# A hybrid decoder block: 128 bytes under the last product's stationary tiles, the first chunk's loads ahead of its gates, and a last norm without GpSimd

## The chip, the cores and the metric

The kernel runs on one core of one Trainium2 chip. The metric is the device time of one execution in microseconds (us), lower is better. A run of this kernel has three timed executions, 1505.19, 1507.73 and 1509.2 us, with a median of 1507.73 us; one more execution was profiled, and it took 1503.95 us.

Names of the engines in what follows: PE is the matrix engine (PEld its loads of the stationary operand), DVE the vector engine, ACT the scalar engine, POOL is GpSimd, SP the engine that here only issues transfers. A "product" is one PE matmul instruction.

## The reference

One decoder layer on 512 rows of 1024 float32 values: a mixer (windowed attention beside gated linear attention), then a retrieval layer over 16384 experts, with a modulated norm before each and a plain norm at the end. The change touches the expert layer's second half and the final norm.

```python
q = (h @ wq).reshape(B, S, PEER_HEADS, 2, PEER_QDIM // 2)
sub_scores = jnp.einsum('bshpk,hpnk->bshpn', q, subkeys)
top_v, top_i = lax.top_k(sub_scores, PEER_TOPK)            # 16 of 128 keys, twice per head
... best 16 of 256 candidate pairs -> expert (row number), gates (softmax)
ub = jnp.take(u, eb, axis=0)                               # 128 rows of u per token
hid = jax.nn.gelu(jnp.einsum('tkd,td->tk', ub, xb), approximate=False) * gb
vb = jnp.take(v, eb, axis=0)                               # 128 rows of v per token
return jnp.einsum('tk,tkd->td', hid, vb)
...
x = x + gate2 * peer_ffn(h2, ...)
return rms_norm(x, final_norm_w)                           # x * rsqrt(mean(x*x) + 1e-6) * w
```

## The kernel before

**Two ways to the experts.** The 512 tokens are four blocks of 128. For the last block (number 3, `GB`) the kernel gathers the rows of u and v that each token asks for: POOL issues 128 indirect transfers of 512 KB for u (`gather_u`, tile `gu`) and 128 for v (`gather_v`, tile `gv`), and DVE turns each into a row of `hid` or adds it to `gacc`. For the other three blocks (`DENSE`) it is dense: PE multiplies all 16384 rows of u with the tokens, in 128 chunks of 128 experts (the U part, tile `ph`, 24 products of 352 columns per chunk), ACT applies gelu and stores it to DRAM (`gsp`), and the gates of the chosen experts, scattered into a dense matrix (`Gd`, written in 24 pieces through `gs`), are multiplied on. The V part then adds, chunk by chunk, the products of (gelu x gate) with the chunk's 128 rows of v into six PSUM banks `acc`, one for each of three blocks and two halves of 512 columns.

**Float32 by parts.** Each operand is split in a high and a low part (`...h`, `...l`, written by ACT and by DVE), and one float32 product is three PE products in `mm3`: high by high (line 70), high by low (71) and low by high (72). In the V part the stationary operand is a 128x128 slice of `Ah` or `Al` (gelu x gate, four tiles each, 1536 bytes per partition and tile), and the moving operand is one half, 512 columns, of `vc..h` or `vc..l`. A V chunk is therefore 3 blocks x 2 halves x 3 = 18 products, and each is preceded by its own load of the stationary operand.

**Order of the V part.** A list `xs` names the chunks left to do: the last odd U chunks, one ahead of every second V chunk as far as they go, then V chunks alone. `prep(i)` puts the work on ACT, DVE and POOL that chunk i needs (multiply gelu by gate at line 1289, split, gather as many rows as `due[i]` asks for), two steps ahead of PE. `loads(i)` issues transfers on SP's queue ahead of need: v (1 MB for two chunks, line 1221), gelu (`gel` for two even chunks, 1227; `geo` for one odd chunk, 1234), gates (`gr`, 1.5 MB for eight chunks, 1244; the first in two halves, one on SP and one on POOL, 1242). A queue issues in order, so a transfer that has to wait holds those behind it. The engines' orders are as written in the code from here on (`manual_schedule`); no planner moves them.

**Where tiles stand.** The tiles of the V part come from the pool `dn` at the upper end of a partition's 229,376 bytes, in which each new name takes the next place. In the built program the four `Ah` tiles start at byte 204,640 and `Al` at 210,784; `vc..h` stands from 88,032 and `vc..l` from 104,416 in another pool.

**The end.** `close_half` (lines 1331 to 1334) takes one PSUM bank: two DVE instructions, then a square with a sum on ACT. `root` makes the mean and the logarithm/exponential root of it (two DVE, two ACT instructions of one column), `refine` a Newton step (DVE, one column), `finish` scales by root and weight and stores. Block 3 is closed while PE still works, at steps counted from `LAST_G`; the last four chunks run block by block, so that block 0 can be closed first, then 1, then 2. Block 1's scaling was on ACT and its multiplication with the weight `fwb` on POOL (line 1441); block 2's on DVE (1444, 1446) ahead of its scale.

Of the kernel before, what the change touches and what calls it, by code (L numbers as in the profile page):

```python
# [7 lines left out]
F32 = mybir.dt.float32  # L8
# [4 lines left out]
AF = mybir.ActivationFunctionType  # L13
OP = mybir.AluOpType
# [3 lines left out]
P = 128  # L18
# [29 lines left out]
def peer_block_kernel(ctx: ExitStack, tc: tile.TileContext, a: dict, out: bass.AP):  # L48
    nc = tc.nc
# [8 lines left out]
    def raw(shape, name):  # L58
        return st.tile(shape, F32, tag="raw", bufs=3, name=name)
# [17 lines left out]
    def rstd_of(pool, ss, n, w, name):  # L77
        m = pool.tile([P, w], F32, name=name + "m", tag="rsm", bufs=2)
        y = pool.tile([P, w], F32, name=name + "y", tag="rsy", bufs=2)
        t = pool.tile([P, w], F32, name=name + "t", tag="rst", bufs=2)  # L80
        nc.vector.tensor_scalar(m, ss, 1.0 / n, EPS, op0=OP.mult, op1=OP.add)
        nc.scalar.activation(y, m, AF.Ln)
        nc.scalar.activation(y, y, AF.Exp, scale=-0.5)
        nc.vector.tensor_tensor(t, y, y, OP.mult)
        nc.vector.tensor_tensor(t, t, m, OP.mult)
        nc.vector.tensor_scalar(t, t, -0.5, 1.5, op0=OP.mult, op1=OP.add)
        nc.vector.tensor_tensor(y, y, t, OP.mult)
        return y
# [94 lines left out]
    for L in LW:  # L183
        m = 64 >> L
# [50 lines left out]
    for n in range(NT):  # L235
# [5 lines left out]
        r = rstd_of(frA, ss[:, 0:1], float(D), 1, f"ra{n}")  # L241
# [927 lines left out]
    dn = ctx.enter_context(tc.tile_pool(name="dn", bufs=1, side="right", reuse_waits="tile"))  # L1169
    pacc = ctx.enter_context(tc.tile_pool(name="pacc", bufs=1, space=PSUM, side="right", reuse_waits="tile"))  # L1170
    acc = [pacc.tile([P, 512], F32, name=f"acc{i}") for i in range(2 * len(DENSE))]
    fwb = dn.tile([P, D], F32, name="fwb")
    gacc = dn.tile([P, D], F32, name="gacc")
    vPc = a["vP"].rearrange("(c i) d -> c i d", i=P)
    LEAD, LAST, LAST_G = 8, 4, 121

    rest = [c for c in range(1, P, 2) if c not in AHEAD]
    xs = [("u", c) for c in rest if c <= LEAD]
# [24 lines left out]
    raws = Ring(lambda name: raw([P, 2, D], name), 3)  # L1203
# [14 lines left out]
    def load_v(ring):  # L1218
        c = vrest.pop(0)
        v = ring.take(f"v{c}", step["v", c + 1])  # L1220
        nc.sync.dma_start(v, vPc[c:c + 2].rearrange("c i d -> i c d"))
        vraw[c], vraw[c + 1] = v[:, 0], v[:, 1]

    def load_gel():
        c = grest.pop(0)
        t = gels.take(f"gel{c}", step["v", c + 2])
        nc.sync.dma_start(t, gsp[c // 4, 0].rearrange("c p t -> p c t"))
        for j in range(2):
            gel[c + 2 * j] = t[:, j].rearrange("p (g t) -> p g t", g=NGU)
# [6 lines left out]
    def load_gates():  # L1236
        j = jrest.pop(0)
        t = gates_r[j] = grs.take(f"gr{j}", step["v", j * CG + CG - 1])
        flat = lambda h: t[h].rearrange("p g c t -> p g (c t)")
        if j == 0:  # L1240
            for h, eng in ((slice(0, 64), nc.sync), (slice(64, P), nc.gpsimd)):
                eng.dma_start(flat(h), Gd[j, h])
        else:
            nc.sync.dma_start(flat(slice(0, P)), Gd[j])

    def loads(i):
        at = lambda x, n: step[x] <= i + n
        if i == 1:
            load_gates()
            load_v(raws)  # L1250
            load_gel()
        if i < 1:
            return
        while True:
            if vrest and at(("v", vrest[0]), 12) and vraws.free(i):
                load_v(vraws)
            elif vrest and not urest and at(("v", vrest[0]), 9) and raws.free(i):
                load_v(raws)
            elif urest and at(("u", urest[0]), 9) and raws.free(i):
                load_u()  # L1260
            elif grest and at(("v", grest[0]), 9) and gels.free(i):
                load_gel()
            elif orest and at(("v", orest[0]), 9) and odds.free(i):
                load_odd()
            elif jrest and at(("v", jrest[0] * CG), 11) and grs.free(i):
                load_gates()
            else:
                break
# [45 lines left out]
    def spare(name):  # L1314
        return gp.tile([P, D], F32, tag="gr", bufs=GR, name=name)

    def spare2(name):
        return dn.tile([P, D], F32, tag="gr2", bufs=G2, name=name)

    def half(t, q):  # L1320
        return t[:, q * 512:(q + 1) * 512]

    gate2b = h2n
    fin = {}
# [5 lines left out]
    def close_half(n, src, q):  # L1330
        y, xr, ss = fin[n][:3]
        nc.vector.tensor_tensor(half(y, q), src, half(gate2b, q), OP.mult)
        nc.vector.tensor_tensor(half(y, q), half(y, q), half(xr, q), OP.add)
        nc.scalar.activation(half(xr, q), half(y, q), AF.Square, accum_out=ss[:, q:q + 1])

    def root(n):
        ss = fin[n][2]
        m, r = ss[:, 2:3], ss[:, 3:4]
        nc.vector.tensor_tensor(ss[:, 0:1], ss[:, 0:1], ss[:, 1:2], OP.add)
        nc.vector.tensor_scalar(m, ss[:, 0:1], 1.0 / D, EPS, op0=OP.mult, op1=OP.add)  # L1340
        nc.scalar.activation(r, m, AF.Ln)
        nc.scalar.activation(r, r, AF.Exp, scale=-0.5)
        fin[n] += [m, r]

    def refine(n):
        m, r = fin[n][3:5]
        t = fin[n][2][:, 4:5]
        nc.vector.tensor_tensor(t, r, r, OP.mult)
        nc.vector.tensor_tensor(t, t, m, OP.mult)
        nc.vector.tensor_scalar(t, t, -0.5, 1.5, op0=OP.mult, op1=OP.add)  # L1350
        nc.vector.tensor_tensor(r, r, t, OP.mult)

    def store(n, q, t, eng=None):
        (eng or nc.sync).dma_start(out[n * P:(n + 1) * P, q * 512:(q + 1) * 512], half(t, q))
# [63 lines left out]
    for b in DENSE[1:]:  # L1418
        for q in range(2):
            v_matmuls(last, (b,), (q,))  # L1420

    n0, n1, n2 = DENSE
    x0, x1 = fin[n0], fin[n1]
    for n, y, xr in ((n0, spare("y0"), x0), (n1, spare2("y1"), x1)):
        fin[n] = [y, xr, dn.tile([P, 5], F32, tag=f"sm{n}", bufs=1, name=f"sm{n}")]
    open_block(n2, spare2("y2"), spare("xf2"))
    w2 = spare("w2")
    close_half(n0, acc[0], 0)
    close_half(n0, acc[1], 1)
    close_half(n1, acc[2], 0)  # L1430
    root(n0)
    refine(n0)
    finish(n0)
    close_half(n1, acc[3], 1)
    close_half(n2, acc[4], 0)
    root(n1)
    refine(n1)
    y1, r1 = fin[n1][0], fin[n1][4]
    for q in range(2):
        nc.scalar.activation(half(y1, q), half(y1, q), AF.Copy, scale=r1)  # L1440
        nc.gpsimd.tensor_tensor(half(y1, q), half(y1, q), half(fwb, q), OP.mult)
        store(n1, q, y1)
    y2 = fin[n2][0]
    nc.vector.tensor_tensor(half(w2, 0), half(y2, 0), half(fwb, 0), OP.mult)
    close_half(n2, acc[5], 1)
    nc.vector.tensor_tensor(half(w2, 1), half(y2, 1), half(fwb, 1), OP.mult)
    root(n2)
    refine(n2)
    r2 = fin[n2][4]
    nc.scalar.activation(half(w2, 0), half(w2, 0), AF.Copy, scale=r2)  # L1450
    store(n2, 0, w2, nc.scalar)
    nc.vector.tensor_scalar(half(w2, 1), half(w2, 1), r2, None, op0=OP.mult)
    store(n2, 1, w2)


# [57 lines left out]
```

## Time and profile before

| what | us |
|---|---|
| median of the timed executions | 1507.73 |
| the profiled execution, its own time | 1503.95 |
| its span, first to last instruction | 1502.2 |
| PE busy in the span | 1451.1 |
| DVE busy | 1262.3 |
| ACT busy | 681.3 |
| POOL busy | 533.8 |
| first V product starts at | 799.59 |
| last V product starts at | 1490.01 |

A "page" is the profile's summary of this one execution; "views" are answers of the trace behind it. In a row of instructions the first number is the start in the span, the second how long it took, then engine, line, kind, "what is written <- what is read" and in brackets the idle time of that engine just before and what ended it. Products are pipelined: each is recorded as longer than the step to the next one's start, and the step is what counts. In a row of a view by stretches stand, for each engine, busy time and number of instructions, then the clock that PE was granted (1.00 is full), the busy share of the transfer engines and what they moved.

### The profile page before, as it was taken

The numbers are of one execution on the slowest core, as the hardware profiler recorded it, in microseconds if no ns is written. First come the engines' busy times: TensorE is split into PE (matmuls) and PEld (weight loads), VectorE is DVE, ScalarE is ACT, GpSimd is POOL, SyncE is SP. The second block draws the span as 40 slices with busy tenths as digits, with TensorE's granted clock in tenths as the row PEclk, the third lists the DMA queues.
The fourth block names the chain that finished last, engine by engine and source line by source line (L and its number), as shares of the span: only waits on it lengthen the run. The fifth ranks groups of instructions, "written<-read, shape, count | busy, mean of one in ns | idle before, by whom it ended". The sixth has DMA issues, their size and how long they took to land.

```text
span 1502.2 us, 24546 instructions
## 1 busy us (share of the span) xinstructions
PE 1451.1 (97%) x9387; PEld 1281.2 (85%) x9387; DVE 1262.3 (84%) x2422; ACT 681.3 (45%) x1073; POOL 533.8 (36%) x360
## 2 busy tenths in 40 slices
PE   4999999899999999999999999999999999999996
PEld 3787877788999999999998888888888888888885
DVE  7578757689999999899956888888888888988886
ACT  5445576533444565566643333333333333433343
POOL 1000000145516444122324555555665656533210
PEclk9999999999999999999999999999999999999998
DMA  9253435353356999799999999999999999999941
GB/s 348 104 212 114 170 94 215 135 187 135 111 184 216 330 347 344 253 318 328 332 294 399 409 364 407 361 372 356 391 372 364 357 404 354 406 407 406 363 161 70
DMA packets 165893, 431.63 MB, mean 287 GB/s; under 512 B 12032, under 2 KB 83984, under 8 KB 153360
## 3 DMA queue, kind: packets, MB, share of 16 engines
q1 hardware_dynamic: 109920, 261.81, 47.7%
q0 software_dynamic: 41552, 151.80, 27.2%
q10 hardware_dynamic: 14304, 16.46, 3.1%
q8 instruction: 73, 1.20, 0.3%
q14 instruction: 44, 0.36, 0.1%
HBM read 385.48 MB, written 44.50 MB: 286 GB/s over the span
## 4 chain that ended last, share of the span: by engine, by line
PE 90%; DVE 4%; ACT 3%; DMA 2%; issue 1%; SPq 0%; DVEq 0%; ACTq 0%
PE acc L71 12%; PE acc L72 12%; PE acc L70 12%; PE ph L70 10%; PE ph L72 10%; PE ph L71 10%; PE pg L929 4%; PE pq L70 2%; PE pq L72 2%; PE pq L71 2%; DMA gel<-gsp 1%; PE pj L72 1%; PE pj L70 1%; PE pj L71 1%; DVE macc L275 1%; PE pn L70 1%
## 5 line engine op out<-in xcount | busy, mean ns | idle before, releaser
L1004 POOL DMA_INDIRECT gu<-in_u_dram,ix_u x128 | 197.1, 1540 | 252.5 <-DVE gu L1014 103.8
L1039 POOL DMA_INDIRECT gv<-in_vP_dram,ix_v x128 | 190.6, 1489 | 177.2 <-DVE gacc L1044 112.1
L1044 DVE SCALAR_TENSOR_TENSOR gacc<-gv,hg,gacc 128x1024 f32<-128x1024 f32 x127 | 162.5, 1280 | 0.2
L1014 DVE SCALAR_TENSOR_TENSOR gu<-gu,h2n 128x1024 f32<-128x1024 f32 x128 | 155.4, 1219 | 2.8 <-DMA gu<-in_u_dram,ix_u 2.8
L706 ACT ACTIVATE ge<-ph 128x352 f32<-128x352 f32 x128 | 57.9, 452 | 202.2 <-PE ph L72 164.1
L970 POOL DMA_INDIRECT spr<-in_u_dram,spix x32 | 72.4, 2263 | 106.4 <-DVE spr L975 69.4
L1293 ACT ACTIVATE Ah<-gr 128x384 fp32r<-128x384 f32 x128 | 66.5, 520 | 93.9 <-DVE gr L1289 93.9
L1094 POOL IOTA iot<- 128x256 bf16 x1 | 1.5, 1542 | 281.5 <-DVE h2Tl L681 281.5
L931 ACT ACTIVATE gs<-pg 128x512 f32<-128x512 f32 x96 | 95.1, 1114 | 0.0
L922 DVE TENSOR_TENSOR o<-o,gp 128x3072 bf16<-128x3072 bf16 x48 | 83.9, 1752 | 0.0
L929 PE MATMUL pg<-o,o 128*128 128x128 bf16 x1152 | 73.6, 219 | 0.0
L929 PEld LDWEIGHTS <-o 128*128 128x128 bf16 x1152 | 66.3, 97 | 5.4
L1302 DVE TENSOR_TENSOR Al<-gr,Ah 128x384 fp32r<-128x384 f32 x128 | 70.6, 551 | 0.0
L906 DVE TENSOR_TENSOR o<-iot,t 128x2048 bf16<-128x2048 bf16 x48 | 58.3, 1220 | 11.1 <-PE pg L929 11.1
L218 DVE SCALAR_TENSOR_TENSOR macc<-wa,scs,macc 128x1024 f32<-128x1024 f32 x28 | 39.3, 1403 | 4.3 <-DMA wa<-in_w_ada_dram 3.9
L975 DVE SCALAR_TENSOR_TENSOR spr<-spr,xs 128x1024 f32<-128x1024 f32 x32 | 39.0, 1220 | 3.6 <-DMA spr<-in_u_dram,spix 3.5
L1289 DVE TENSOR_TENSOR gr<-gel,gr 128x352 f32<-128x352 f32 x64 | 33.2, 519 | 9.4 <-DMA gel<-gsp 9.4
L71 PE MATMUL pq<-h2Tl,wq_0h 128*128 128x512 f32 (+1 forms) x80 | 27.9, 349 | 1.2 <-DVE h2Tl L681 1.2
L70 PE MATMUL pq<-h2Th,wq_0h 128*128 128x512 f32 (+1 forms) x80 | 28.0, 352 | 1.0 <-ACT qha L769 1.0
L71 PE MATMUL pq<-h2Tl,wq_1h 128*128 128x512 f32 (+1 forms) x80 | 28.2, 352 | 0.0
L72 PE MATMUL pq<-h2Th,wq_1l 128*128 128x512 f32 (+1 forms) x80 | 28.1, 351 | 0.0
L70 PE MATMUL pq<-h2Th,wq_1h 128*128 128x512 f32 (+1 forms) x80 | 28.0, 349 | 0.0
(2587 smaller groups left out, 5042.5 us busy)
## 6 DMA issues: line engine op xcount, KB each, us to landing
u<-in_uT_dram SPq DMA_DIRECT2D x64, 1024.0 KB
v<-in_vP_dram SPq DMA_DIRECT2D x64, 1024.0 KB
Gd<-gs SPq DMA_DIRECT2D x23, 1024.0 KB
gr<-Gd SPq DMA_DIRECT2D x15, 1536.0 KB
wa<-in_w_ada_dram SPq DMA_DIRECT2D x20, 1024.0 KB
gsp<-ge ACTq DMA_DIRECT2D x84, 176.0 KB
gel<-gsp SPq DMA_DIRECT2D x32, 352.0 KB
wi<-in_w_in_dram SPq DMA_DIRECT2D x9, 1024.0 KB
```

The costliest lines, as they stand in the source:

```text
L70: nc.tensor.matmul(acc, lh, rh, start=start, stop=False)
L71: nc.tensor.matmul(acc, lh, rl, start=False, stop=False)
L72: return nc.tensor.matmul(acc, ll, rh, start=False, stop=stop)
L922: nc.vector.tensor_tensor(o2, o12[:, :, 1, None].to_broadcast([P, H, 3, P, 2]), gp3[:, g0:g0 + H, :, None].to_broadcast([P, H, 3, P, 2]), ...
L929: nc.tensor.matmul(pt[:, i, :], o12[:, g, 0, :, r], o2[:, g, m, :, r], start=(m == 0), stop=(m == 2))
L931: nc.scalar.activation(gs[:, :, t0 + 4 * f:t0 + 4 * f + 4].rearrange("p b a -> p a b"), pt, AF.Copy)
L970: nc.gpsimd.indirect_dma_start(out=sp[j], out_offset=None, in_=a["u"], in_offset=bass.IndirectOffsetOnAxis(ap=sp["ix"][:, j:j + 1], axis=0))
L1004: nc.gpsimd.indirect_dma_start(out=ur, out_offset=None, in_=a["u"], in_offset=bass.IndirectOffsetOnAxis(ap=ix_u[:, s:s + 1], axis=0))
L1014: nc.vector.scalar_tensor_tensor(ur, ur, 1.0, h2n, op0=OP.mult, op1=OP.mult, accum_out=hid[:, s:s + 1])
L1039: nc.gpsimd.indirect_dma_start(out=vr, out_offset=None, in_=a["vP"], in_offset=bass.IndirectOffsetOnAxis(ap=ix_v[:, s:s + 1], axis=0))
L1044: nc.vector.scalar_tensor_tensor(gacc, vr, hg[:, s:s + 1], gacc, op0=OP.mult, op1=OP.add)
L1302: nc.vector.tensor_tensor(grp(Al), A, grp(Ah), OP.subtract)
```

## The change

1. **Place.** A tile `gap` of 32 float32 (128 bytes) is added to the pool `dn`. In the built program the `Ah` tiles then start at 204,512 and the `Al` tiles at 210,656, 128 bytes lower than before; `vc..h` and `vc..l` stay where they were. Because of point 2, `gel` and `gr` also change places in the pool.
2. **Order of the first loads.** At step 1 `loads` issued the first gates, then the first v, then the first gelu. Now it issues gelu, v, gates.
3. **The last norm.** `refine` multiplies twice in one instruction. Block 0's `root` stands ahead of block 1's first `close_half`, and block 1's `root` ahead of block 2's first. Block 1 is weighted on DVE into a new tile `w1` and scaled on ACT, which also stores it; POOL has no part in it any more.
4. **`LAST_G`** is 122 instead of 121: the 256 gathers are spread up to V chunk 122, and block 3's closing steps come one chunk later.

```diff
-    LEAD, LAST, LAST_G = 8, 4, 121
+    LEAD, LAST, LAST_G = 8, 4, 122
...
     def loads(i):
         if i == 1:
+            load_gel()
+            load_v(raws)
             load_gates()
-            load_v(raws)
-            load_gel()
...
     def refine(n):
-        nc.vector.tensor_tensor(t, r, r, OP.mult)
-        nc.vector.tensor_tensor(t, t, m, OP.mult)
+        nc.vector.scalar_tensor_tensor(t, r, r, m, op0=OP.mult, op1=OP.mult)
         nc.vector.tensor_scalar(t, t, -0.5, 1.5, op0=OP.mult, op1=OP.add)
         nc.vector.tensor_tensor(r, r, t, OP.mult)
+    def weighted(n, q, w):
+        nc.vector.tensor_tensor(half(w, q), half(fin[n][0], q), half(fwb, q), OP.mult)
+    def scaled(n, q, w):
+        nc.scalar.activation(half(w, q), half(w, q), AF.Copy, scale=fin[n][4])
+        store(n, q, w, nc.scalar)
...
+    dn.tile([P, 32], F32, name="gap")
...
+    w1 = spare2("w1")
     close_half(n0, acc[0], 0)
     close_half(n0, acc[1], 1)
+    root(n0)
     close_half(n1, acc[2], 0)
-    root(n0)
     refine(n0)
     finish(n0)
     close_half(n1, acc[3], 1)
+    root(n1)
     close_half(n2, acc[4], 0)
-    root(n1)
+    weighted(n1, 0, w1)
     refine(n1)
-    for q in range(2):
-        nc.scalar.activation(half(y1, q), half(y1, q), AF.Copy, scale=r1)
-        nc.gpsimd.tensor_tensor(half(y1, q), half(y1, q), half(fwb, q), OP.mult)
-        store(n1, q, y1)
-    nc.vector.tensor_tensor(half(w2, 0), half(y2, 0), half(fwb, 0), OP.mult)
+    scaled(n1, 0, w1)
+    weighted(n1, 1, w1)
+    scaled(n1, 1, w1)
+    weighted(n2, 0, w2)
     close_half(n2, acc[5], 1)
-    nc.vector.tensor_tensor(half(w2, 1), half(y2, 1), half(fwb, 1), OP.mult)
+    weighted(n2, 1, w2)
     root(n2)
     refine(n2)
-    nc.scalar.activation(half(w2, 0), half(w2, 0), AF.Copy, scale=r2)
-    store(n2, 0, w2, nc.scalar)
-    nc.vector.tensor_scalar(half(w2, 1), half(w2, 1), r2, None, op0=OP.mult)
+    scaled(n2, 0, w2)
+    nc.vector.tensor_scalar(half(w2, 1), half(w2, 1), fin[n2][4], None, op0=OP.mult)
     store(n2, 1, w2)
```

PE's instructions stand in the same order before and after; only addresses differ. Two places on other engines matter.

The first is SP's queue at the start of the V part, as a difference (u are the last U chunks' weights, `gr` the gates of chunks 0 to 7, `v` and `gel` rows of v and gelu for the first chunks; the numbers at the names' ends are buffers):

```order
 L1215 DMA u_8935<-in_uT_dram 128x2048
-L1242 DMA gr_8946<-Gd 64x3072
-L1221 DMA v_8949<-in_vP_dram 128x2x1024
-L1227 DMA gel_8951<-gsp 128x2x352
+L1227 DMA gel_8946<-gsp 128x2x352
+L1221 DMA v_8948<-in_vP_dram 128x2x1024
+L1242 DMA gr_8950<-Gd 64x3072
 L1221 DMA v_8953<-in_vP_dram 128x2x1024
 L1221 DMA v_8955<-in_vP_dram 128x2x1024
```

The three transfers have swapped their outer two, so that gelu and v no longer stand behind the gates, which must wait for the last piece of `Gd`; the other half of the gates stays where it was on POOL's queue.

The second is DVE at the very end, from the first half of block 2 (`acc_8927`) on. Before (`y_14829` and `sm_14832` are block 2, `sm_14828` block 1):

```order
L1332 TENSOR_TENSOR y_14829<-acc_8927,h2n 128x512
L1333 TENSOR_TENSOR y_14829<-y_14829,xf_14830 128x512
L1339 TENSOR_TENSOR sm_14828<-sm_14828 128x1
L1340 TENSOR_SCALAR sm_14828<-sm_14828 128x1
L1348 TENSOR_TENSOR sm_14828<-sm_14828 128x1
L1349 TENSOR_TENSOR sm_14828<-sm_14828 128x1
L1350 TENSOR_SCALAR sm_14828<-sm_14828 128x1
L1351 TENSOR_TENSOR sm_14828<-sm_14828 128x1
L1444 TENSOR_TENSOR w_14833<-y_14829,fwb 128x512
L1332 TENSOR_TENSOR y_14829<-acc_8928,h2n 128x512
L1333 TENSOR_TENSOR y_14829<-y_14829,xf_14830 128x512
L1446 TENSOR_TENSOR w_14833<-y_14829,fwb 128x512
```

And now, with the same names (`w_14834` is the new `w1`; lines 1348 to 1350 are `refine`, 1353 is `weighted`):

```order
L1339 TENSOR_TENSOR sm_14828<-sm_14828 128x1
L1340 TENSOR_SCALAR sm_14828<-sm_14828 128x1
L1332 TENSOR_TENSOR y_14829<-acc_8927,h2n 128x512
L1333 TENSOR_TENSOR y_14829<-y_14829,xf_14830 128x512
L1353 TENSOR_TENSOR w_14834<-y_14826,fwb 128x512
L1348 SCALAR_TENSOR_TENSOR sm_14828<-sm_14828 128x1
L1349 TENSOR_SCALAR sm_14828<-sm_14828 128x1
L1350 TENSOR_TENSOR sm_14828<-sm_14828 128x1
L1353 TENSOR_TENSOR w_14834<-y_14826,fwb 128x512
L1353 TENSOR_TENSOR w_14833<-y_14829,fwb 128x512
L1332 TENSOR_TENSOR y_14829<-acc_8928,h2n 128x512
L1333 TENSOR_TENSOR y_14829<-y_14829,xf_14830 128x512
```

Block 1's root has moved ahead of block 2's first half, the Newton step is one instruction shorter, and two multiplications with the weight, which POOL made before, stand on DVE ahead of block 2's second half.

More of the change, by code (lines that the diff above doesn't have):

```diff
@@ L1434, in peer_block_kernel @@
     close_half(n1, acc[3], 1)
+    root(n1)
     close_half(n2, acc[4], 0)
-    root(n1)
+    weighted(n1, 0, w1)
     refine(n1)
-    y1, r1 = fin[n1][0], fin[n1][4]
-    for q in range(2):
-        nc.scalar.activation(half(y1, q), half(y1, q), AF.Copy, scale=r1)
-        nc.gpsimd.tensor_tensor(half(y1, q), half(y1, q), half(fwb, q), OP.mult)
-        store(n1, q, y1)
-    y2 = fin[n2][0]
-    nc.vector.tensor_tensor(half(w2, 0), half(y2, 0), half(fwb, 0), OP.mult)
+    scaled(n1, 0, w1)
+    weighted(n1, 1, w1)
+    scaled(n1, 1, w1)
+    weighted(n2, 0, w2)
     close_half(n2, acc[5], 1)
-    nc.vector.tensor_tensor(half(w2, 1), half(y2, 1), half(fwb, 1), OP.mult)
+    weighted(n2, 1, w2)
     root(n2)
     refine(n2)
-    r2 = fin[n2][4]
-    nc.scalar.activation(half(w2, 0), half(w2, 0), AF.Copy, scale=r2)
-    store(n2, 0, w2, nc.scalar)
-    nc.vector.tensor_scalar(half(w2, 1), half(w2, 1), r2, None, op0=OP.mult)
+    scaled(n2, 0, w2)
+    nc.vector.tensor_scalar(half(w2, 1), half(w2, 1), fin[n2][4], None, op0=OP.mult)
     store(n2, 1, w2)
```

## The prediction

> **What bounds the kernel now.** I read the page's busy times first, then the chain that ended last, and then the steps between products in PE's rows in order of time.
>
> ```profile
> PE 1451.1 (97%) x9387; PEld 1281.2 (85%) x9387; DVE 1262.3 (84%) x2422; ACT 681.3 (45%) x1073; POOL 533.8 (36%) x360
> PE 90%; DVE 4%; ACT 3%; DMA 2%; issue 1%; SPq 0%; DVEq 0%; ACTq 0%
> PE acc L71 12%; PE acc L72 12%; PE acc L70 12%; PE ph L70 10%; PE ph L72 10%; PE ph L71 10%; PE pg L929 4%; PE pq L70 2%; PE pq L72 2%; PE pq L71 2%; DMA gel<-gsp 1%; PE pj L72 1%; PE pj L70 1%; PE pj L71 1%; DVE macc L275 1%; PE pn L70 1%
> ```
>
> PE makes 90% of the chain, and the V products (`acc`) 36% of it: about 540 us. What a V product costs PE sets the time, as long as transfers and DVE keep up.
>
> **Part 1, the place of the stationary tiles.** All products here with 512 moving columns do the same arithmetic. Below are, from the rows in order of time, the starts of a product and of the eighteenth after it in four groups (`pj`, `pw`, `pq`, `acc`):
>
> ```profile
> 72.50 0.39 PE L70 MATMUL pj<-hTh,wi_0h 128*128 128x512 f32 x1
> 76.58 0.39 PE L70 MATMUL pj<-hTh,wi_1h 128*128 128x512 f32 x1
> ...
> 246.34 0.39 PE L70 MATMUL pw<-wo2000h,ah 128*128 128x512 f32 x1
> 250.46 0.39 PE L70 MATMUL pw<-wo2000h,ah 128*128 128x512 f32 x1
> ...
> 337.31 0.39 PE L70 MATMUL pq<-h2Th,wq_0h 128*128 128x512 f32 x1
> 341.44 0.39 PE L70 MATMUL pq<-h2Th,wq_1h 128*128 128x512 f32 x1
> ...
> 1205.30 0.39 PE L70 MATMUL acc<-vc66h,Ah 128*128 128x512 f32 x1
> 1209.48 0.40 PE L70 MATMUL acc<-vc67h,Ah 128*128 128x512 f32 x1
> 1209.72 0.39 PE L71 MATMUL acc<-vc67l,Ah 128*128 128x512 f32 x1
> ...
> 1213.68 0.32 PE L70 MATMUL ph<-h2Th,uc77h 128*128 128x352 f32 x1
> ```
>
> Eighteen products take 4.08 us in `pj`, 4.12 in `pw`, 4.13 in `pq`, and 4.20 in a V chunk (4.18 in one that follows a U chunk). What differs is where the operands stand. By the built program's addresses, divided by 512, moving and stationary operand leave 160 and 160 in `pj`, 480 and 160 in `pw`, 288 and 480 in `pq`, 480 and 352 in `acc`. Stationary less moving, again by 512: 0, 192, 192, 384. `pw` and `pq` have no remainder in common but the same difference, and the same time within 0.01 us. So I read it thus: while a product streams, the next one's stationary tile is read, and the two reads disturb each other by the difference of their addresses.
>
> The change makes the difference 256. If the pattern repeats every 256 bytes, that is `pj`'s 0, and a chunk takes 4.08. If it repeats every 512 only, 256 lies between 192 (4.13) and 384 (4.20), by a straight line at 4.15. In units of 256 the groups stand at 0, 192 and 128 with 4.08, 4.13, 4.20: the worst is the one farthest from 0, as a repeating pattern would have it. I take 4.08. Of the 128 chunks 40 follow a U chunk (44 odd chunks are left for this part, four of them run ahead of it): now 88 x 4.20 + 40 x 4.18 = 536.8 us, then 128 x 4.08 = 522.2 us, **-14.6 us**. The bounds are -5.6 (4.15) and, if the guess on addresses is wrong altogether, 0 or a loss, priced below.
>
> The Trainium skill speaks against this part: its page TensorE: Matmul & The Clock Gate, section Step-by-step: what each phase is for, says that PE has two independent read ports and that loading the next stationary tile takes no read bandwidth from the running product. By that rule part 1 brings nothing and the sum is that of the rival "no effect"; the four times above are what the rule leaves unexplained.
>
> Can the rest keep up? While PE only ran V chunks and gathers were at their densest:
>
> ```profile
> DMA packets 65643, 243.09 MB, mean 380 GB/s; under 512 B 5979, under 2 KB 16159, under 8 KB 61251
> ...
> 1300.00:1400.00 100.00, 100.00 (x431) 80.42 (x430) 87.93 (x121) 35.35 (x49) 39.80 (x32) 1.00 1.03 404
> ...
> ACT vc6h L1290 <- DMA v<-in_vP_dram: 4.7, 1, 4.7
> ```
>
> From 800 to 1440 us 243 MB move at 380 GB/s; 14.6 us less asks for 389, and 404 was held over 100 us. The last row is ACT's longest wait for a transfer there, once, early. DVE, 88% busy in the second row, goes to about 90%. Neither becomes the bound.
>
> **Part 2, the first loads.** From the chain, the rows of SP, POOL, DVE and PE, and the view by stretches of 1 us:
>
> ```profile
> 773.23 6.03 DMA Gd<-gs
> 779.32 0.49 SPq L1242
> ...
> 791.94 0.94 POOL L1039 DMA_INDIRECT gv<-in_vP_dram,ix_v  x1 [2.08 <-DMA gr<-Gd]
> ...
> 795.03 1.06 ACT L1290 ACTIVATE vc0h<-v 128x1024 fp32r<-128x1024 f32 x1 [4.33 <-DMA v<-in_vP_dram]
> ...
> 798.46 0.53 DVE L1289 TENSOR_TENSOR gr<-gel,gr 128x352 f32<-128x352 f32 x1 [9.40 <-DMA gel<-gsp]
> ...
> 797.39 0.32 PE L71 MATMUL ph<-h2Tl,uc9h 128*128 128x352 f32 x1
> 797.55 0.32 PE L72 MATMUL ph<-h2Th,uc9l 128*128 128x352 f32 x1
> 799.59 0.49 PE L70 MATMUL acc<-vc0h,Ah 128*128 128x512 f32 x1 [1.72 <-ACT Ah L1293]
> 806.03 0.39 PE L70 MATMUL acc<-vc1h,Ah 128*128 128x512 f32 x1
> ...
> 802.00:803.00 1.00, 1.00 (x4) 0.71 (x4) 1.00 (x3) 0.88 (x1) 0.00 (x0) 0.50 1.04 418
> ```
>
> The gates wait for the last piece of `Gd` until 779.32; v and gelu stand behind them and land at 795 and 798. PE, free at 797.71 (797.55 and a step of 0.16), starts at 799.59, 1.88 us late, and its first chunk takes 6.44 us instead of 4.18, because low parts come late and, after the idle time, the granted clock is 0.50: 2.26 us more. Together 4.1 us.
>
> Now gelu and v go out right behind the last u, before 773, and the gates are last. Both halves had landed by 791.94, when POOL's next gather was let go. The 1.4 MB moved ahead can hold up `Gd` and with it the gates, at 404 GB/s by 3.5 us, to 795.4. From gates to PE it is 799.59 - 798.46 = 1.13 us, so PE could start at 796.5, before it is free. **-4.1 us**; the bound is 0, if `Gd` is held up some 3 us more. POOL's gathers behind its half of the gates move by the same 3.5 us at most.
>
> On the clock, the same page of the Trainium skill, section HAM oscillation — how this bites in real kernels, lets PE idle for about 3.4 us before it is slowed; by that rule only the idle 1.88 us and the late parts were to be had here, but the row at 802 shows the slower clock after 1.88 us.
>
> **Part 3, the last norm.** DVE's rows, with one of ACT and POOL each:
>
> ```profile
> 1482.07 0.69 DVE L1332 TENSOR_TENSOR y<-acc,h2n 128x512 f32<-128x512 f32 x1 [0.73 <-PE acc L72]
> 1486.71 0.68 DVE L1332 TENSOR_TENSOR y<-acc,h2n 128x512 f32<-128x512 f32 x1
> 1488.04 0.68 DVE L1332 TENSOR_TENSOR y<-acc,h2n 128x512 f32<-128x512 f32 x1
> 1489.37 0.15 DVE L1339 TENSOR_TENSOR sm<-sm 128x1 f32<-128x1 f32 x1
> 1490.57 0.16 DVE L1348 TENSOR_TENSOR sm<-sm 128x1 f32<-128x1 f32 x1 [0.86 <-ACT sm L1342]
> 1491.22 0.69 DVE L1444 TENSOR_TENSOR w<-y,fwb 128x512 f32<-128x512 f32 x1
> 1491.84 0.68 DVE L1332 TENSOR_TENSOR y<-acc,h2n 128x512 f32<-128x512 f32 x1
> 1492.55 1.41 DVE L1333 TENSOR_TENSOR y<-y,xf 128x512 f32<-128x512 f32 x1
> 1493.99 1.64 DVE L1446 TENSOR_TENSOR w<-y,fwb 128x512 f32<-128x512 f32 x1
> 1496.78 0.15 DVE L1350 TENSOR_SCALAR sm<-sm 128x1 f32<-128x1 f32 x1
> 1496.97 0.16 DVE L1351 TENSOR_TENSOR sm<-sm 128x1 f32<-128x1 f32 x1
> 1497.17 0.49 DVE L1452 TENSOR_SCALAR w<-w,sm 128x512 f32<-128x512 f32 x1
> ...
> 1490.02 0.19 ACT L1334 ACTIVATION_READ_ACCUMULATOR xf<-y 128x1 f32 x1
> ...
> 1492.15 2.94 POOL L1441 TENSOR_TENSOR y<-y,fwb 128x512 f32<-128x512 f32 x2 [56.29 <-ACT y L1440]
> ```
>
> From 1482.07 to the last scale at 1497.17 DVE never waits for PE, so its own list is the path. While POOL works, two instructions that take 0.69 elsewhere take 1.41 and 1.64: +1.7 us, gone without POOL. Three Newton steps lose an instruction each (0.19, 1496.78 to 1496.97): -0.6. Waits for ACT's logarithm behind blocks 0 and 1 (0.86 us in block 1's row, taken for both) are covered by a `close_half` (1.33, 1486.71 to 1488.04): -1.7. Added: two weightings at 0.62 (1491.22 to 1491.84), +1.2; and `root` of blocks 0 and 1 now comes at once behind the half whose square it needs, which is done about 0.85 us after DVE (1490.21 against 1489.37): +0.9 for block 1 and +0.4 for block 0, where 0.73 was a wait for PE anyway. Sum **-1.5 us**; bounds 0 and -2.5. ACT's two scales and stores of block 1 fit before block 2's last square.
>
> **Part 4, `LAST_G`.** One chunk more for the gathers; block 3's closing falls into DVE's waits for PE-freed tiles. 0, at worst +0.5.
>
> **Sum** against the profiled execution: 1503.95 - 14.6 - 4.1 - 1.5 = 1483.7. The timed median stands 3.8 us above it, so I predict 1507.73 - 20.2 = **1487.5 us**.
>
> **Rivals.**
> *Half an effect.* The pattern has a period of 512: a chunk at 4.13 to 4.15, -8.3 to -5.6 instead of -14.6. For it: only `pj` shows 4.08, and its difference is 0 and not 256. About 1495.
> *No effect.* The steps follow the order of products and not addresses: `acc` changes its bank every three products. Against it: each group is steady, and `pw` and `pq`, with different tiles, agree. Only parts 2 and 3 count, -5.6: 1502.1. The same time results if transfers hold V at its old pace.
> *Slower.* A difference of 256 is the worst case of a period of 512: every step at 0.24 us, the longest that rows of V products show (1209.48 to 1209.72 and the like, now every other step), makes a chunk 4.32 and the V part +16.2, net +10.6: 1518. It decides from 4.24 on (4.195 + 5.6 / 128). Against it: from 0 to 192 the loss is 0.05 of the 0.12 at 384.
> *The gap stays.* `Gd` is held up by the loads moved ahead: 1491.6.
>
> **Chances.** Forecast 0.45; half 0.25; none 0.15; slower 0.08; gap stays 0.07. 0.3% is 4.5 us, about what a measurement can tell here. Faster: 0.45 + 0.25 + 0.07 and 0.06 of "none", which lies close to the line: 0.83. Same 0.09, slower 0.08. Range 1483 (the forecast less 1.0 to part 3's bound and 2.5 by which the lowest of the timed runs lies under their median) to 1503 ("none", with 0.5 for part 4); above it lie "slower" and part of "none".
>
> **What would show it.** Part 1: 18 V products in 4.08 us. Part 2: no idle time before the first `acc`, clock 1.00 there. Part 3: lines 1333 and 1353 at 0.69 throughout and the last scale some 1.5 us nearer to the last product. A V chunk at 4.20 or more refutes part 1, a DVE wait for `gr` beyond 797 part 2.

## The result, and the profile after

The changed kernel takes **1486.70 us** (median; 1484.27 to 1491.16), the kernel before beside it 1506.49 us (1505.19 to 1509.20). The ratio is 0.987, with a 95% interval from 0.9837 to 0.9902. The forecast was 1487.5 us.

The profiled execution of the changed kernel is its slowest one, 1491.16 us with a span of 1489.40. The two spans therefore differ by 12.8 us only, and the stages show why. The times are read from PE's rows in order of time: the first and last product of a stage.

| stage | before | after | difference | forecast |
|---|---|---|---|---|
| start to first U product (`ph`) | 294.56 | 302.34 | +7.78 | 0 |
| to the last product of the gates (`pg`) | 476.15 | 476.02 | -0.13 | 0 |
| to the first V product (`acc`) | 28.88 | 26.99 | -1.89 | -1.88 |
| to the last V product | 690.41 | 674.11 | -16.30 | -14.6 - 2.26 |
| to DVE's last scale | 7.16 | 5.75 | -1.41 | -1.5 |
| to the end of the span | 5.01 | 4.19 | -0.82 | 0 |

The last four rows are what the change touches, and they sum to -20.42 us; forecast were -20.2. The first row is the part of the program that the change leaves alone. There the two executions were granted different clocks: the column behind the five engines (first kernel after, then before, 10 us each).

```profile
160.00:170.00 10.00, 10.00 (x65) 6.67 (x65) 7.74 (x11) 1.73 (x5) 0.00 (x0) 0.60 0.92 324
...
290.00:300.00 10.00, 7.85 (x50) 7.18 (x50) 2.23 (x3) 3.08 (x6) 1.87 (x2) 0.83 0.00 0
```

```profile
160.00:170.00 10.00, 10.00 (x180) 7.81 (x180) 6.92 (x14) 7.14 (x23) 0.00 (x0) 1.00 0.88 307
...
290.00:300.00 10.00, 10.00 (x80) 10.00 (x79) 5.54 (x31) 4.72 (x7) 2.76 (x2) 1.00 0.41 146
```

Over 120 to 190 and 290 to 300 us the same view's clock is short of 1.00 by 10.3 us after and 3.4 us before (each stretch of 10 us times one less its clock). So some 6.9 of the 7.8 us are this one execution's clock, which also moves the medians of either kernel by a few us (the changed kernel took 1484.27 us at a mean clock of 0.996 and 1491.16 us at 0.991). From here on I compare stages, and totals only where they were timed several times.

**The page.** PE makes 93% of the chain where it made 90%, and no longer waits at the start of the V part. The chain's share of DMA is 1% where it was 2%, and the 17.78 us step of `gel` is no longer in it.

```profile
PE 1441.8 (97%) x9387; PEld 1285.2 (86%) x9387; DVE 1263.0 (85%) x2420; ACT 681.8 (46%) x1073; POOL 530.7 (36%) x358
PE 93%; DVE 3%; ACT 2%; DMA 1%; issue 1%; SPq 0%; DVEq 0%; ACTq 0%
```

**The V part.** In PE's rows a chunk of 18 products takes 4.07 and 4.09 us, where it took 4.20. In the view by stretches (the first pair is PE's busy time and number of products) 443 products fit into 100 us where 431 did. DVE is at 91% and the transfers at 406 GB/s there, and neither holds PE up.

```profile
1298.37 0.39 PE L70 MATMUL acc<-vc84h,Ah 128*128 128x512 f32 x1
1302.44 0.39 PE L70 MATMUL acc<-vc85h,Ah 128*128 128x512 f32 x1
1306.53 0.39 PE L70 MATMUL acc<-vc86h,Ah 128*128 128x512 f32 x1
```
```profile
1300.00:1400.00 100.00, 100.00 (x443) 82.81 (x442) 90.76 (x126) 35.66 (x51) 43.04 (x33) 1.00 1.03 406
```

**The first chunk.** The rows of ACT's queue, SP's queue, DVE and PE, and the clock:

```profile
780.88 0.38 ACTq L934 DMA_DIRECT2D Gd<-gs  x1
...
792.25 0.49 SPq L1242 DMA_DIRECT2D gr<-Gd  x1
...
802.76 0.53 DVE L1289 TENSOR_TENSOR gr<-gel,gr 128x352 f32<-128x352 f32 x1 [6.06 <-DMA gr<-Gd]
...
805.35 0.39 PE L70 MATMUL acc<-vc0h,Ah 128*128 128x512 f32 x1
...
809.45 0.39 PE L70 MATMUL acc<-vc1h,Ah 128*128 128x512 f32 x1
```
```profile
805.00:806.00 1.00, 1.00 (x7) 0.91 (x6) 1.00 (x2) 0.78 (x3) 0.00 (x0) 1.00 1.02 406
```

The row of the first V product has no idle time in brackets, the clock there is 1.00, and the chunk takes 4.10 us instead of 6.44. The gates are now what lands last. `Gd`'s last store is issued at 780.88 and lets the gates go at 792.25, 11.4 us later; before it was 6.1 (773.23 to 779.32). DVE can multiply at 802.76, and by the 1.13 us from there to PE the first product could have started at 803.89: a margin of 1.46 us.

**The end.** DVE's last rows:

```profile
1482.24 0.69 DVE L1333 TENSOR_TENSOR y<-y,xf 128x512 f32<-128x512 f32 x1
1482.96 0.69 DVE L1353 TENSOR_TENSOR w<-y,fwb 128x512 f32<-128x512 f32 x1
1485.21 0.48 DVE L1456 TENSOR_SCALAR w<-w,sm 128x512 f32<-128x512 f32 x1
```

The two instructions that had taken 1.41 and 1.64 us take 0.69. The last scale stands 5.75 us behind the last product (1479.46) where it stood 7.16 behind it (1490.01).

### The profile page after: what moved, and what is told of

It is laid out like the page before. It is cut to its first block, busy times and chain, and to the rows that moved or that the text cites. A ratio compares the mean times of both kernels' runs of the same rounds, so it can differ in the third digit from the quotient of the medians.

```text
span 1489.4 us, 24541 instructions
## 1 busy us (share of the span) xinstructions
PE 1441.8 (97%) x9387; PEld 1285.2 (86%) x9387; DVE 1263.0 (85%) x2420; ACT 681.8 (46%) x1073; POOL 530.7 (36%) x358
## 4 chain that ended last, share of the span: by engine, by line
PE 93%; DVE 3%; ACT 2%; DMA 1%; issue 1%; SPq 0%; DVEq 0%; ACTq 0%
PE acc L71 11%; PE acc L72 11%; PE acc L70 11%; PE ph L70 11%; PE ph L72 11%; PE ph L71 11%; PE pg L929 4%; PE pq L70 2%; PE pq L72 2%; PE pq L71 2%; PE pj L72 1%; PE pj L70 1%; PE pj L71 1%; PE pn L70 1%; PE pn L71 1%; PE sc L395 1%
## 5 line engine op out<-in xcount | busy, mean ns | idle before, releaser
L1004 POOL DMA_INDIRECT gu<-in_u_dram,ix_u x128 | 201.8, 1576 | 242.1 <-PE pg L929 97.2
L1039 POOL DMA_INDIRECT gv<-in_vP_dram,ix_v x128 | 186.0, 1453 | 167.7 <-DVE gacc L1044 109.6
L906 DVE TENSOR_TENSOR o<-iot,t 128x2048 bf16<-128x2048 bf16 x48 | 58.2, 1218 | 10.3 <-PE pg L929 10.3
```

The lines of the kernel that those rows point to most:

```text
L1004: nc.gpsimd.indirect_dma_start(out=ur, out_offset=None, in_=a["u"], in_offset=bass.IndirectOffsetOnAxis(ap=ix_u[:, s:s + 1], axis=0))
L1039: nc.gpsimd.indirect_dma_start(out=vr, out_offset=None, in_=a["vP"], in_offset=bass.IndirectOffsetOnAxis(ap=ix_v[:, s:s + 1], axis=0))
```

## Experiments: each part alone

My theory: the three parts act in three stages and add up, with the place of the tiles as the largest by far. The rival: the gain is that of the loads and the norm, and V's pace follows from something else, such as the order of products.

**The gap alone**, in the kernel before:

```diff
+    dn.tile([P, 32], F32, name="gap")
     n0, n1, n2 = DENSE
```

> The kernel before with one line more: the 128-byte tile `gap` ahead of the V part's stationary tiles. Loads, last norm and LAST_G stay as they were. Theory (a step depends on stationary address less moving address, with a period of 256 bytes): 18 V products take 4.08 us instead of 4.20, and the stretch from the first to the last V product shrinks by some 14 us (690.4 to about 676); the 1.88 us of PE's wait before the first V product and its slow first chunk stay; time about 1492 us, ratio 0.990. Rival (the gain of the change comes from its loads and its norm, steps follow the order of products): steps stay at 4.20, time 1506.

Measured: 1494.28 us, ratio 0.9905 (0.9875 to 0.9935) against 1508.17. First to last V product: 676.14 us, 14.27 less than before. The windows and PE's waits of this kernel:

```profile
1300.00:1400.00 100.00, 100.00 (x443) 82.82 (x442) 90.78 (x126) 35.86 (x51) 41.54 (x33) 1.00 1.03 406
```
```profile
PE acc L70 <- ACT Ah L1293: 3.1, 1, 3.1
```

One line that computes nothing gives the whole pace of 443 products in 100 us. The wait ahead of the first V product stays; here it is 3.1 us and not 1.7, in an execution in which `Gd`'s store let the gates go 7.9 us after its issue instead of 6.1 (775.77 to 783.64). The time stands 2 us above the 1492 expected; in this profile the longer wait is 1.4 us of that.

**The loads alone**, in the kernel before:

```diff
         if i == 1:
-            load_gates()
+            load_gel()
             load_v(raws)
-            load_gel()
+            load_gates()
```

> The kernel before with the three loads of chunk 0 in the new order alone: gelu, v, gates. Theory: PE no longer waits before the first V product, and its first chunk takes 4.2 us instead of 6.4, so the stretch from the last U product's chunk to the second V chunk shrinks by 4.1 us; time about 1502.5 us. What the trace of the change shows already: the last store of block Gd then takes some 5 us longer and the gates land last, at about the time PE comes free, so that up to 1 us of wait may be left. Rival (the wait only moves to the gates): no gain, 1506. V steps stay at 4.20 by either.

Measured: 1502.43 us, ratio 0.9965 (0.9951 to 0.9978). PE has no wait there, the first V product comes 26.99 us behind the last `pg`, and first to last V product is 688.19 us: 1.89 and 2.22, together the 4.1 us forecast. V's pace is untouched:

```profile
1300.00:1400.00 100.00, 100.00 (x430) 80.45 (x429) 87.90 (x121) 35.14 (x49) 39.76 (x33) 1.00 1.03 403
```

Timed it gains 5.7 us, and this fits too: the wait that it removes was 1.88 us in the profile that I had, but 2.23, 3.28 and 3.44 us (the stretch from the last `pg` to the first `acc`, less 26.99) in the other three profiles here that kept the old order. My profile held the shortest of the four.

**The last norm alone**, as the changed kernel with everything else undone:

```diff
-    LEAD, LAST, LAST_G = 8, 4, 122
+    LEAD, LAST, LAST_G = 8, 4, 121
...
-            load_gel()
+            load_gates()
             load_v(raws)
-            load_gates()
+            load_gel()
...
-    dn.tile([P, 32], F32, name="gap")
```

> The kernel before with the new last norm alone (blocks n1 and n2 weighted by DVE and scaled by ACT, a Newton step one instruction shorter). Theory: the 512-column instructions of DVE at the end take 0.69 us throughout (1.41 and 1.64 before), and the stretch from the last product to the end shrinks from 12.2 us by 1.5 to 2.2; time about 1505, which the timing alone can't tell from no change. Rival (the two long DVE instructions have another cause than GpSimd's work beside them): they stay long in their place and nothing is gained.

Measured: 1505.31 us, ratio 0.9975 (0.9957 to 0.9994). From the last product to the end it takes 9.65 us instead of 12.17, of which 1.70 lie ahead of the last scale.

```profile
1494.47 0.69 DVE L1333 TENSOR_TENSOR y<-y,xf 128x512 f32<-128x512 f32 x1
1495.20 0.69 DVE L1353 TENSOR_TENSOR w<-y,fwb 128x512 f32<-128x512 f32 x1
```

The three timed gains, 13.9, 5.7 and 2.9 us, sum to 22.5; the whole change gained 19.8 (14.8 to 24.6 by its interval). They add up within what can be measured.

**`LAST_G` alone undone**, in the changed kernel:

```diff
-    LEAD, LAST, LAST_G = 8, 4, 122
+    LEAD, LAST, LAST_G = 8, 4, 121
```

> The changed kernel with LAST_G at 121 as before. Theory: nothing changes beyond 0.5 us in the stretch from the first to the last V product (674.1 to 675.7 in the kernels with V products at 227 ns) and in the one from there to the end (9.9). Rival (block 3's closing must give way to the faster V part): a wait of PE at the end, and 1 us or more longer.

Measured: 1484.73 us (one execution). First to last V product 674.11 us and from there 9.94 us, both to the last digit what the changed kernel has. The rival falls: block 3's closing is hidden with 121 as with 122.

## Experiments: what in the place counts

Each of these changes two numbers in the changed kernel, the padding of `hg` (which moves the pool of `vc..h` and `uc..h`) and the size of the gap (which moves `Ah` and `Al`). The first one, as an example of the form:

```diff
-    hg = h2p.tile([P, P + 48], F32, name="hg")[:, :P]
+    hg = h2p.tile([P, P + 0], F32, name="hg")[:, :P]
...
-    dn.tile([P, 32], F32, name="gap")
+    dn.tile([P, 16], F32, name="gap")
```

> The changed kernel with the padding of `hg` cut from 48 to 0 elements and the gap from 128 to 64 bytes. The moving tiles of the V part then stand 192 bytes lower, its stationary tiles 64 higher than in the change: stationary less moving is 0 by 512 (256 in the change). In the U part stationary less moving goes from 192 to 0 by 512. V part, theory of the difference: 4.08 us for 18 products as in the change, though both operands stand elsewhere; rival (what counts is the stationary tile's own place, 224 by 512): another step. U part, 352 moving columns, 160 ns a product now: if it follows the same pattern as 512 columns (4.13 at 192, 4.08 at 0), about 158 ns, and 3072 products gain 6 us: 1480; if 352 columns are already at their limit, or the other way round (256 columns take 117.8 ns at 192 and 120 at 0), 0 to +7 us.

In the others padding and gap are 16 elements and no gap, 48 and 64 bytes, 32 and none, none and none, 56 and 96 bytes:

> The changed kernel without the gap, and with the padding of `hg` cut from 48 to 16 elements: the stationary tiles of the V part stand where they stood before the change (352 by 512), and the moving tiles 128 bytes lower (352). Stationary less moving is 0 by 512, as in the kernel with 64 bytes of gap and no padding. Theory (the difference counts): V products at 226.8 to 227.0 ns, no slower than with the gap. Rival (the stationary tile's own place counts): 233 ns, as before. U part: stationary less moving is 64 by 512; 160.0 ns at 192 and 160.6 at 0, so 159 to 162.

> The changed kernel with half the gap: 64 bytes. Stationary less moving in the V part is 320 by 512, 64 by 256. It has been 227 ns at 0 and 256, 229 at 192, 233 at 384 (128 by 256). Theory (a period of 256, worst in the middle): between 227 and 233 ns, and the same as at 64 in the run without padding and gap. Rival (a threshold: any distance from 0 costs the whole): 233 ns. The U part is untouched: 160.0.

> The changed kernel without the gap, and with the padding of `hg` cut to 32 elements. Stationary less moving is 448 by 512 in the V part (192 by 256) and 128 by 512 in the U part. Theory (a period of 256): V products at 229 ns, as the groups pq and pw at 192; U products, at the worst distance, above 161 ns (by the ratio of V's 233 to 229 some 163), which would make the U part 8 us longer. Rival (period 512): V nearer to 384's 233 than to 229 is excluded only by this run; U within 0.6 ns of 160.0, as it was between 192 and 0.

> The changed kernel without the gap and without the padding of `hg`. Stationary less moving is 64 by 512 in the V part and 0 in the U part. Theory (a period of 256): V products take the same time as in the run with half the gap (320 by 512), within 0.5 ns. Rival (period 512): they differ from it. U: 160.6 ns, as in the earlier run at 0.

> The changed kernel with the padding of hg at 56 elements and the gap at 96 bytes. Stationary less moving stays 256 by 512 in the V part (227 ns) and goes to 224 by 256 in the U part, pq and pw. U products took 160.0 ns at 192, 160.3 to 160.6 at 0, 160.1 at 64, 165.4 at 128. Theory (352 columns are at their least everywhere but near 128): 159 to 161 ns. Rival (there is a place with less): under 158.5, which over 3072 products would be 4.6 us and more. pq and pw, 229 ns at 192 and 227 at 0: between them.

The view by stretches while only V chunks run, one row from each kernel: padding 0 and gap 64; 16 and none; 48 and 64; none and none; 32 and none.

```profile
1300.00:1400.00 100.00, 100.00 (x443) 82.81 (x442) 90.15 (x124) 35.65 (x51) 40.64 (x34) 1.00 1.03 405
```
```profile
1300.00:1400.00 100.00, 100.00 (x443) 82.81 (x442) 90.14 (x125) 36.57 (x52) 42.46 (x34) 1.00 1.03 406
```
```profile
1300.00:1400.00 100.00, 100.00 (x431) 80.55 (x430) 87.86 (x122) 35.45 (x50) 41.58 (x33) 1.00 1.03 405
```
```profile
1300.00:1400.00 100.00, 100.00 (x430) 80.60 (x429) 87.86 (x122) 35.55 (x50) 41.24 (x33) 1.00 1.03 405
```
```profile
1300.00:1400.00 100.00, 100.00 (x439) 82.06 (x438) 90.10 (x126) 36.81 (x52) 44.59 (x34) 1.00 1.03 405
```

The first two kernels have their operands in different places, and the second has its stationary tiles where the slow kernel before had them; both run at 443. Their difference is 0 by 512, the changed kernel's 256, and the pace is one: **the difference counts, by 256 bytes**. The third and fourth, at 320 and 64 by 512, agree as well, and both are as slow as before: half the gap would have gained nothing, as the rival of that run had it.

Moving the pools also moved `pw`, `pq` and `ph`, so one table can be made of it all. It holds the mean time in ns from one product's start to the next one's, worked out from PE's rows of each kernel (2263 steps for `acc`, 184 for `pw`, 274 of 512 columns for `pq`, 2977 of 352 columns for `ph`; steps more than an eighth above the group's median, where PE was stalled or slowed, are left out), by stationary less moving address:

| by 256 | `acc` | `pw` | `pq` | `ph`, 352 columns |
|---|---|---|---|---|
| 0 | 226.9, 226.8, 227.3, 227.4 (changed; padding and gap 0, 64; 16, 0; 56, 96) | 228.1 (32, 0) | 228.1 (0, 0 and 0, 64) | 160.6, 160.2 (0, 64; 0, 0) |
| 64 | 233.2, 233.2 (48, 64; 0, 0) | 233.3 (16, 0) | 233.1 (16, 0) | 160.2 (16, 0) |
| 128 | 233.1 (before) | 232.6, 232.7 (0, 0; 0, 64) | 232.4 (32, 0) | 163.9 (32, 0) |
| 160 | - | 233.3 (56, 96) | - | - |
| 192 | 228.9 (32, 0) | 229.4 (changed) | 229.4 (changed) | 160.0 (changed) |
| 224 | - | - | 233.3 (56, 96) | 160.0 (56, 96) |

In the last kernel `pw` stands at 160 and not, as I had expected, at 224: its moving operand lies in the pool that the padding moves, where `pq` has its stationary one. Nor do the two lie between 227 and 229 ns there; they take 233.3.

Three groups of products in three pools, with other tiles and other neighbours, take the same time at the same difference, within 1.3 ns at 0 and within 0.7 at 64, 128 and 192. So it isn't the order of products, which never changed. That two reads disturb each other is my reading of it: the runs show that the step follows the difference, and not what happens inside. As all products of a group have one difference, they don't tell either whether a product's own stationary tile counts or the next one's. The Trainium skill, TensorE: Matmul & The Clock Gate, section Step-by-step: what each phase is for, has two independent read ports, so that loading the next stationary tile costs the running product nothing; these runs disagree with it by up to 6.4 ns a product (226.8 against 233.2).

The shape is not what I had drawn, though. I took 128 to be the worst place, with a smooth way back to 0; 64, 160 and 224 are as bad as 128, and 192 is a second low place. And 352 columns have another shape: 160.0 to 160.6 ns at all places but 128 (163.9), where the U part (first U product to the last `pg`) becomes 9.4 us longer (485.37 against 476.02 us). For 256 columns (186 steps of `pq`) the shape is a third one: 119.8 ns at 0, 118.6 at 128, 117.2 at 192, 116.9 at 224, and the least, 115.4, at 64, where 512 columns are slow. The view by stretches of the U part shows the loss of 352 columns at 128, changed kernel first, then padding 32 without a gap:

```profile
505.00:565.00 60.00, 60.00 (x527) 58.79 (x526) 58.50 (x63) 35.65 (x47) 26.75 (x15) 1.00 1.01 345
```
```profile
505.00:565.00 60.00, 60.00 (x502) 58.88 (x501) 59.60 (x65) 34.58 (x45) 25.61 (x16) 1.00 1.01 352
```

As totals the kernels took 1488.25 us (0, 64; ratio 0.9879, 0.984 to 0.9917), 1489.57 (16, 0), 1503.68 (48, 64), 1502.16 (32, 0), 1503.32 (0, 0) and 1484.64 (56, 96), all but the first in one execution. None of them beats the changed kernel by more than its own spread: it already has the V part at its lowest place and the U part at its lowest too. What is left by the table is `pq` and `pw` at 192 instead of 0, about 1 ns for 458 steps, under 1 us.

## Experiments: the two smaller parts

**GpSimd's share in the end.** The kernel before, without GpSimd's two multiplications:

```diff
         nc.scalar.activation(half(y1, q), half(y1, q), AF.Copy, scale=r1)
-        nc.gpsimd.tensor_tensor(half(y1, q), half(y1, q), half(fwb, q), OP.mult)
         store(n1, q, y1)
```

> The kernel before without GpSimd's two multiplications at the end: block n1's second half of the norm, its weighting by fwb, is left out, and nothing takes its place. Theory (GpSimd's work beside DVE makes DVE's two rows long): lines 1333 and 1446 at 0.69 where they took 1.41 and 1.64, and the stretch from the last product to the end 1.7 us shorter than before's 12.2: 10.5. Rival (the two rows are long for another reason, such as ACT's reads of the same tiles): they stay at 1.4 and 1.6.

Measured: from the last product to the end 9.83 us instead of 12.17, and DVE's two rows:

```profile
1493.56 0.69 DVE L1333 TENSOR_TENSOR y<-y,xf 128x512 f32<-128x512 f32 x1
1494.28 0.69 DVE L1445 TENSOR_TENSOR w<-y,fwb 128x512 f32<-128x512 f32 x1
```

GpSimd's work beside DVE had made them long. The last scale stands 5.63 us behind the last product, the rewritten norm's 5.75: taking GpSimd away is worth 1.53 of the 7.16 us, and all else that the new norm does to DVE's list comes to +0.12 (-0.17 where it was put alone into the kernel before, 5.46 us). The Trainium skill, Perfetto Trace Analysis, section Optimizing Scalar/DVE Operations, says that GpSimd and DVE share a read port, so that moving work from one to the other might not help; these rows agree, 1.41 and 1.64 us with it and 0.69 without. There is a second gain that I had not priced. From the last scale to the end of the span it takes 4.20 us here and 4.19 in the changed kernel, against 5.01 before. It isn't the stores: in all three kernels the transfers of the last two start 1.34 or 1.35 us behind the last scale and take 1.52 us. What differs is the program's closing line, where each engine has an instruction `DRAIN` and the engines then wait for each other by semaphores (`EVENT_SEMAPHORE`). In the kernel before (number of instructions, the least, median and longest duration in ns, and the starts of the first and the last in us):

```profile
L1509 POOLq DRAIN  x3: 40/102/8677, 1492.7 to 1501.9; - x3
L1509 SPq DRAIN  x3: 7/7/7, 1500.5 to 1501.7; - x3
L1509 POOLq EVENT_SEMAPHORE  x4: 17/17/17, 1501.4 to 1502.1; - x4
```

GpSimd's first `DRAIN` starts at 1492.7 and takes 8.68 us, until 1501.4. That is 6.3 us behind the end of its last multiplication, which the row in the prediction puts at 1495.09, and 0.9 us behind SP's first `DRAIN`; its first semaphore comes only then. In the changed kernel GpSimd's long `DRAIN` ends 50 us before the span does, and its first semaphore comes at 1488.7, 0.1 us behind SP's first `DRAIN` at 1488.6. So GpSimd's work costs about 0.8 us a second time, at the very end. Why its `DRAIN` lasts so long stays open.

**Which of gelu and v had to go ahead.** In the changed kernel:

```diff
             load_gel()
-            load_v(raws)
             load_gates()
+            load_v(raws)
```

> The changed kernel with chunk 0's loads in the order gelu, gates, v instead of gelu, v, gates. Theory (gelu behind the gates was what let PE wait, v behind them only made the first chunk slow): no wait for gelu, Gd's last store takes less than the 11.3 us of the change since 0.5 MB less stands beside it, the gates land earlier; v lands later than in the change, and the price is a slow first chunk: the stretch from the first to the last V product 0 to 2 us longer than 674.1, PE's start 26.99 us after the last pg product as in the change. Rival (Gd's store is held up by the u loads anyway): the gates land as late as in the change, v behind them, and PE waits for v by 1 to 3 us.

Measured: 1486.09 us (one execution). `Gd`'s store lets the gates go 8.7 us after its issue (773.90 to 782.56), the gates are there for DVE at 794.07, and still PE's first V product is 27.90 us behind the last `pg` instead of 26.99. First to last V product is 675.06, 0.95 longer than in the changed kernel. ACT's and PE's rows, and the clock:

```profile
797.81 1.06 ACT L1290 ACTIVATE vc0h<-v 128x1024 fp32r<-128x1024 f32 x1 [6.41 <-DMA v<-in_vP_dram]
798.77 0.50 ACT L1293 ACTIVATE Ah<-gr 128x384 fp32r<-128x384 f32 x1
...
799.33 0.49 PE L70 MATMUL acc<-vc0h,Ah 128*128 128x512 f32 x1 [0.75 <-ACT Ah L1293]
800.18 0.50 PE L71 MATMUL acc<-vc0l,Ah 128*128 128x512 f32 x1 [0.36 <-DVE vc0l L1298]
```
```profile
800.00:801.00 1.00, 0.82 (x3) 0.50 (x4) 1.00 (x4) 0.57 (x1) 0.00 (x0) 1.00 1.02 406
801.00:802.00 1.00, 1.00 (x6) 0.84 (x5) 1.00 (x2) 0.94 (x3) 0.00 (x0) 1.00 1.04 414
```

The profile names `Ah`, whose operand was ready at 794.6. But ACT takes its instructions in order, and `vc0h`, ahead of `Ah`, waits for v until 797.81. So both had to go ahead of the gates: gelu, or nothing can start; v, or ACT stands. The rival that `Gd`'s store is held up anyway isn't settled: it is held for 10.2 to 11.8 us in the nine kernels with gelu and v ahead, for 6.1 to 7.9 in the four with neither, and for 8.7 in this one with gelu alone. So v ahead costs time there; that gelu alone does isn't shown by one run so near to 7.9.

These rows also tell the two costs of the late start apart. With 0.91 us of waiting, and 0.36 more behind it, the clock stays at 1.00 and the first chunk takes 5.05 us (799.33 to 804.38). In the kernel before, with 1.88 us, the clock goes to 0.50 from 801 on and the chunk takes 6.44:

```profile
801.00:802.00 1.00, 1.00 (x4) 0.81 (x3) 1.00 (x2) 0.94 (x3) 0.00 (x0) 0.57 1.02 406
...
803.00:804.00 1.00, 1.00 (x4) 0.81 (x3) 1.00 (x3) 0.62 (x1) 0.00 (x0) 0.50 1.02 406
804.00:805.00 1.00, 1.00 (x5) 0.81 (x4) 1.00 (x2) 0.44 (x1) 0.96 (x1) 0.72 1.03 410
```

With the row at 802 in the prediction the clock is short of 1.00 by 1.71 us over these four (0.43, 0.50, 0.50, 0.28). Less the 0.36 us that the other chunk waits, that is about the 1.4 us by which the two differ. The Trainium skill, TensorE: Matmul & The Clock Gate, section HAM oscillation — how this bites in real kernels, lets PE idle for about 3.4 us before it is slowed. By these runs 1.88 us of waiting with a sparse chunk behind it are enough, and the longer waits of 2.23, 3.28 and 3.44 us cost no more clock: their first chunks took 6.43, 6.13 and 6.09 us.

## Why the prediction was right, point by point

- **Part 1, the place: right, and by the rule given.** Chunks of 4.08 us, forecast 4.08; -14.27 us with the gap alone, forecast -14.6. The rule "by the difference of the addresses, by 256" was a guess from four groups; six more placements of the V part bear it out, and the moves of `pw` and `pq` with them. That two reads collide remains a reading. What was wrong is the picture behind it: the pattern isn't worst at half its period and doesn't fall off smoothly, so the straight line that priced "half an effect" at 4.13 to 4.15, and the sentence "from 0 to 192 the loss is 0.05 of the 0.12 at 384" against the rival "slower", rested on nothing. A guess of 64 bytes by that line would have been wrong by the whole effect.
- **"Half an effect" (period 512), "no effect", "slower": refuted.** 0 and 256 by 512 agree (226.8 and 226.9 ns), 64 and 320 as well (233.2 both). That transfers or DVE would hold V at its old pace is refuted by 443 products in 100 us.
- **Part 2, the loads: right in size, -4.1 us in the stages, by the two terms named.** `Gd`'s hold-up was taken as 3.5 us at most and was 5.3 (11.4 instead of 6.1). The estimate put PE's possible start 25.8 us behind the last `pg` (796.5 less 770.72), in fact it was 25.5 (803.89 less 778.36); PE was free at 26.99. That these agree is luck: the gates were let go 1.8 us later than assumed, and landed 10.5 us after that (792.25 to 802.76) where they had taken 12.6 (779.32 to 791.94). The rival "the gap stays" was 1.5 us away in this profile. That the old wait differs between executions, from 1.88 to 3.44 us, could not be seen in one profile; timed, this part is worth 5.7 us.
- **Part 3, the norm: the sum right, one term missed.** -1.41 up to the last scale, forecast -1.5; GpSimd's contention -1.53, forecast -1.7; the Newton steps, waits and weightings together -0.17 to +0.12, forecast +0.2. The step that failed is that the sum ended at the last scale: behind it the end no longer waits for GpSimd's closing `DRAIN`, which gained 0.82 more.
- **Part 4: right, 0.**
- **The sum.** -20.2 forecast, -20.42 in the stages that the change touches, -19.8 between the medians. That the total came within 1 us of the forecast is partly luck: one execution's front end alone differs by 7.8 us. The lower end of the range is 1484.0 by its own terms (1487.5 less 1.0 and 2.5), not 1483, and the rival's -8.3 is -8.2 (536.8 less 128 x 4.13).

## What to carry to other kernels

Where products with a stationary load each set the pace, compare the steps of all groups of the same shape before blaming the order or the transfers: if they differ, list stationary less moving address by 256 and try the difference of the fastest group, since 128 bytes of empty tile bought 14 us here. Measure the place, don't interpolate it: 64 bytes bought nothing, and another width of products has another pattern. And where one load is moved ahead, look at every engine's queue behind it: gelu alone was not enough, because ACT splits v ahead of the gates.

## What was unexpected of the hardware

- The step of a 512-column product by the difference of its operands' addresses has two low places (0 and 192 by 256: 226.8 to 228.1 and 228.9 to 229.4 ns) between high ones (64, 128, 160, 224: 232.4 to 233.3). Why 192 is low and its neighbours are not stays open; so do the shapes for 352 columns, flat at 160 ns but for 163.9 at 128, and for 256, lowest at 64 (115.4).
- A product's own place, or that of its stationary tile, made no difference beyond 0.6 ns (`acc` with its stationary tile at 288, 224, 352 and 256 by 512, all with difference 0 by 256: 226.8, 226.9, 227.3 and 227.4).
- A wait of 0.91 us ahead of the V part left the clock at 1.00; one of 1.88 us brought 0.50 for about 3.4 us (1.71 us lost at half the clock).
- GpSimd's closing `DRAIN` ended 6.3 us behind its last multiplication (1495.09 to 1501.4) and held up the end of the program by about 0.8 us.
